# A hybrid decoder trunk: where the branch-gate projections run, beside the RWKV scan or behind it

## The chip, the cores and the metric

The kernel runs on one core of a Trainium2 chip. The metric is the device time of one execution in microseconds. Engines are named as in the profile: PE (TensorE matmul), PEld (TensorE weight load), DVE (VectorE), ACT (ScalarE), POOL (GpSimd), SP (the engine that issues the DMAs).

## The reference

Two layers on 1024 tokens of width 1024 (float32), then a final RMSNorm. In each layer one input projection feeds three causal mixers of width 512 and three branch gates of width 1024; the branches are multiplied by their gates, summed, projected and added to the residual:

```python
proj = h @ w_in
pool_u, pool_g, q, k, v, ret_g, rw, rw_g, gate_logits = jnp.split(proj, points, axis=-1)
o_pool = causal_pool_mixer(pool_u, pool_w, pool_scale) * jax.nn.silu(pool_g)
o_ret = retention(q, k, v, positions, ret_norm_g) * jax.nn.silu(ret_g)
o_rwkv = rwkv7_time_mix(rw, ...) * jax.nn.silu(rw_g)
branches = jnp.stack([o_pool, o_ret, o_rwkv], axis=2)
y = jnp.einsum('btnw,nwd->btnd', branches, w_branch)
gates = jax.nn.sigmoid(gate_logits.reshape(B, T, N_BRANCHES, D))
merged = jnp.sum(gates * y, axis=2)
return x + gate * (merged @ w_out)
```

The RWKV mixer carries a 64x64 state per head through the sequence: `S = S*w + (S a) b + v k`, read out by `r`. It has 8 heads, and is the only part that is serial over the whole sequence.

## The kernel before

Everything is kept transposed, channels on the 128 partitions and tokens along the free dimension, in two halves of 512 tokens. The dense products are computed as three float32r products each (high by high, high by low, low by high), so the input projection of one **item**, 128 output channels of all 1024 tokens, is 2 halves x 8 input tiles x 3 = 48 matmuls of 128x512, all written to the tag `acc` (three PSUM banks). Items are named `lora`, `k`/`r`/`v` (the RWKV inputs of one pair of heads; three together are `RW(i)`), `rq`/`rk`/`rv`/`rg` (retention of one head, `RT(i)`), `pu`/`pg` (one pool group, `PL(g)`), `wg` (RWKV's SiLU gate), `gate n d` (branch gate n, output tile d: 24 per layer, `GT`), `br n d` (branch product for two output tiles, 48 matmuls, `BR`) and `out`.

The RWKV mixer is done for a pair of heads at a time, four pairs a layer, in the generator `rwkv_task`: `prepare` and `scores` for each half (elementwise work on DVE and ACT, small products on PE, into `BK`, `AR`, `G`), the inversion of 32x32 triangles on DVE (`invert`, L924), small products that combine them (`m1`, `m2`, L972 to L993), and then 16 steps of 64 tokens (L1000). A step goes PE (`two<-S,AR`, L1010), DVE (`xst`, L1020), PE (`ch<-xst,G`, L1026), DVE (`Z`, L1027), PE (`ch<-Z,BKt`, L1029), DVE (`S`, L1032), and the next step needs the new `S`. `prog[(l, i)]` is unset until pair i's scores are done, then counts its steps. The pairs run one after the other.

Two orders decide what stands beside what. The **program order** is made while the kernel is traced: small tasks sit in lanes (`norm`, `post`, `rwkv`, `mix`, `ada`), each with a due time on an estimated clock; `mm1` traces the dense matmuls one by one, each advances the clock, and after each `pump` (L415) lets every lane advance whose due time has come. So a scan step's small products stand in the program between as many dense matmuls as the estimate says that its other engines need. On top of this the **framework's scheduler** orders each engine's instructions: in its own model of time it takes the earliest line of the program whose operands and buffers are ready, so that later instructions can move ahead into a hole. On the chip each engine runs its instructions in that order.

Which dense item comes next is said by the planner `plan_layer` (L471), asked one item ahead by `wprep` (L512), which also loads and splits the weights (`wr`, then `wh` on ACT and `wl` on POOL, three buffers each). In the kernel before it yields `lora` and `RW(0)`, then as soon as pair `done` has begun its steps `RW(done+1)` and `RT(done)`, pool items as `done` grows, and in between, whenever none of these may come yet, items of the list `pre`: 24 branch-gate items. Such an early gate item goes through `evac` (L1147): tanh on ACT into `gsg`, and a store to `gd` in DRAM. Gate items that were not reached come behind the scan.

Behind the scan (`merge`, L499, consumed from L1511) the list `seq` is worked off without its early items. A gate item there goes straight from PSUM into a tile `gs` (15 buffers, borrowed from the tags `ri`, `rk`, `vp`, `cs`); early gates are loaded back into such tiles by `prefetch` (L1489). A `br` item multiplies its product with the gate and adds it to `mrg`; its operand, the branch's output, is loaded and split by `load_o` (L1468, tiles `ol`, `oG`, `olo`). Then `out` follows.

Of the kernel before, what the change touches and what calls it, by code (L numbers as in the profile page):

```python
# [54 lines left out]
def RW(h):  # L55
    return [("k", h), ("r", h), ("v", h)]


def RT(h):
    return [("rq", h), ("rk", h), ("rv", h), ("rg", h)]  # L60


def PL(g):
    return [("pu", g), ("pg", g)]


def GT(n, *ds):
    return [("gate", n, d) for d in ds]


def BR(n, *ds):
    return [("br", n, d) for d in ds]
# [24 lines left out]
def trunk_kernel(ctx, tc, xT, cvec, pos, vecs, consts, w_ada, w_all, pool_w, lora_w, out):  # L97
# [15 lines left out]
    def gtile(s):  # L113
        return gp.tile([P, 32 * P + 8], F32, tag="G", name=nm(s))
# [3 lines left out]
    def nm(s):  # L118
        uid[0] += 1
        return f"{s}_{uid[0]}"  # L120
# [34 lines left out]
    def r8(s):  # L155
        return rp.tile([P, 2048], F32, tag="r8", name=nm(s))
# [153 lines left out]
    names = ("norm", "post", "rwkv", "mix", "ada")  # L310
    lanes = {k: deque() for k in names}
    due = {k: 0.0 for k in names}
    clock = [0.0]
# [55 lines left out]
    def advance(k):  # L369
        q = lanes[k]  # L370
        if not q:
            return False
        settle()
        try:
            dt = next(q[0])
        except StopIteration:
            q.popleft()
            dt = 0.0
        due[k] = max(due[k], clock[0]) + (dt or 0.0)
        return True  # L380
# [34 lines left out]
    def pump():  # L415
        for k in names:
            while lanes[k] and due[k] <= clock[0] and advance(k):
                pass
# [34 lines left out]
    prog = {}  # L453
# [5 lines left out]
    def kept(l):  # L459
        return l + 1 == L  # L460

    def out_order(l, part):
        return (2, 3, 0, 4, 5, 1, 6, 7) if kept(l) and part else range(8)
# [3 lines left out]
    def plan():  # L467
        for l in range(L):
            yield from ((l, it) for it in plan_layer(l))

    def plan_layer(l):  # L471
        yield from [("lora",)] + RW(0)
        pools = deque(PL(i) for i in range(4))
        pre = deque(GT(0, *range(8)) + GT(1, 0, 1, 4, 5, 6, 7) + GT(2, 2, 3, 4, 5, 6, 7, 0, 1) + GT(1, 2, 3))
        late = deque([("wg", 0), ("wg", 1), ("wg", 2)])
        done = 0
        while done < 4 or prog.get((l, 3), 0) < 13 or pools or halves[l] < 15:
            if done < 4 and prog.get((l, done), -1) >= 0:
                done += 1
                if done < 4:  # L480
                    yield from RW(done)
                yield from RT(done - 1)
            elif pools and 4 - len(pools) <= done and len(lanes["mix"]) < 2:
                yield from pools.popleft()
            elif pre or late:
                q = late if late and (done == 4 and prog.get((l, 3), -1) >= 0 or not pre) else pre
                it = q.popleft()
                early[l].add(it)
                yield it
            elif pools:  # L490
                yield from pools.popleft()
            elif done < 4:
                done += 1
                if done < 4:
                    yield from RW(done)
                yield from RT(done - 1)
            else:
                break
        yield ("merge",)  # L499
        seq = GT(1, 2, 3) + BR(0, 0, 2, 4, 6) + [("wg", 0), ("wg", 1)]  # L500
        seq += GT(1, 0, 1) + BR(1, 0, 2) + GT(1, 4, 5) + BR(1, 4)
        seq += [("wg", 2), ("wg", 3)] + GT(1, 6, 7) + BR(1, 6)
        seq += GT(2, 0, 1) + BR(2, 0) + GT(2, 2, 3) + BR(2, 2) + GT(2, 4, 5, 6, 7) + BR(2, 4, 6)
        yield from [it for it in seq if it not in early[l]]
        for part in range(2 + (l + 1 == L)):
            yield from [("out", d, part) for d in out_order(l, part)]
# [4 lines left out]

    def wprep(big=False):  # L512
        for l, it in planner:
            if it != ("merge",):
                break
            wready.append((it, None))
        else:
            return
        t = None
        if it[0] == "out" and it[1] >= 2 and kept(l):  # L520
            if it[2]:
                wready.append((it, keep_w[it[1]]))
                return
            if it[1] < 6:
                t = r8("wout")
            else:
                if it[1] == 6:
                    keep_w["G"] = gtile("wG")
                t = keep_w["G"][:, 2048 * (it[1] - 6) : 2048 * (it[1] - 5)]
        elif big:  # L530
            t = r8("wbig")
        parts = []
        for j in range(2):
            if t is not None:
                o = j * D
                hi, lo = t[:, o : o + HF].bitcast(F32R), t[:, o + HF : o + D].bitcast(F32R)
            else:
                hi = wp.tile([P, HF], F32R, tag="wh", name=nm("wh"), bufs=3)
                lo = wp.tile([P, HF], F32R, tag="wl", name=nm("wl"), bufs=3)
            raw = wp.tile([P, HF], F32, tag="wr", name=nm("wr"), bufs=3)  # L540
            nc.sync.dma_start(out=raw, in_=w_all[l, ITEMS.index(it[:2] if it[0] == "out" else it), j])
            split(raw, hi, lo)
            parts.append((hi, lo))
        if it[0] == "out":
            keep_w[it[1]] = parts
        wready.append((it, parts))
# [14 lines left out]
    def split(src, hi, lo, eng=nc.gpsimd):  # L561
        nc.scalar.copy(hi, src)  # L562
        eng.tensor_tensor(lo, src, hi.bitcast(F32), op=ALU.subtract)  # L563
# [723 lines left out]
    with tc.manual_schedule(engines={ET.PE, ET.DVE, ET.Activation, ET.Pool}):  # L1287
# [108 lines left out]
        both(6, V)  # L1396
        both(7, V)
        wprep(True)
        wprep()
        mms(0, 6)  # L1400
        mms(0, 7)
# [7 lines left out]
    for i in range(3):  # L1409
        evac(FIRST[i], acc6[1][i], 1)  # L1410
    wprep()
    setup_rest()
    add("mix", rope_tables())
    late_ada = [(0, g) for g in (6, 7)] + [(1, g) for g in range(8)]

    for l in range(L):
# [10 lines left out]
        def in_tile2(ws):  # L1427
            pss = [acc_ps(), acc_ps()]
            for j in range(2):
                for h in range(2):  # L1430
                    mm3(pss[h], ws[j], hs[h][4 * j : 4 * j + 4], j == 0, j == 1)
            return pss
# [9 lines left out]
                    evac(it, in_tile(ws, h), h)  # L1442
        while wready[0][0] != ("merge",):
            it, ws = wready.popleft()
            wprep()
            for h, ps in enumerate(in_tile2(ws)):
                evac(it, ps, h)
# [63 lines left out]
        while wready[0][0][0] != "out":  # L1511
            it, ws = wready.popleft()
# [49 lines left out]
        for part, (h, sl) in enumerate(parts):  # L1562
# [3 lines left out]
            for i, d in enumerate(out_order(l, part)):  # L1566
                it, ws = wready.popleft()
# [147 lines left out]
```

## Time and profile before

| | before |
|---|---|
| median of 2 runs | 2431.43 us (2431.26 to 2431.59) |
| profiled execution, span | 2431.3 us |
| PE busy | 2353.2 us (97%), 13312 matmuls |
| DVE, POOL, ACT busy | 1313.5, 820.8, 799.9 us |
| DMA | 220.51 MB, 28.5% of 16 engines |
| stores to `gd`, loads from it | 74 and 74, of 256 KB |

The profiled execution's span and its runs' times agree within 0.3 us, so spans and times can be compared directly. In the rows of the profile a line number is that of the kernel; L445 is the helper that every matmul goes through, so matmuls are told apart by the tiles they write and read, and not by line. `x` counts instructions; behind the bar stand the union of their busy time, the mean duration of one in ns, and the idle time of the engine ahead of them with what ended it. The 74 stores are 37 items of the 48 in two layers: 11 gate items came behind the scan already.

### The profile page before, as it was taken

The page shows a single profiled execution, that of the slowest core. Times are in us where ns is not written, and L with a number is a line of the kernel's source. Part 1 is how long each engine was busy: PE and PEld are TensorE (multiplying, and loading weights), DVE is VectorE, ACT ScalarE, POOL GpSimd, SP SyncE. Part 2 cuts the span into 40 slices and gives each one's busy share as a digit, 9 for nine tenths or more (in the row PEclk, how much of TensorE's full clock was granted, in tenths as well). Part 3 has the DMA queues.
Part 4 walks back from the last instruction along what each step waited for, and adds up shares of the span by engine and source line. Part 5 has one row for each costly group of instructions (what it writes and reads, how often), then busy time and mean ns, then how long its engine had stood idle before and what let it go on. Part 6 is the DMA issues. An engine that isn't in the chain of part 4 may idle for free. (4 is left out here: it accounts for less than half of the span.)

```text
span 2431.3 us, 34768 instructions
## 1 busy us (share of the span) xinstructions
PE 2353.2 (97%) x13312; PEld 1925.5 (79%) x13312; DVE 1313.5 (54%) x2564; ACT 799.9 (33%) x1481; POOL 820.8 (34%) x729
## 2 busy tenths in 40 slices
PE   5989999999999999999999999999999999999998
PEld 4768878878887888777877887888787888878888
DVE  7665477367468542457455646745644674322244
ACT  5542333333234223112453324323322323212243
POOL 4321232232232424364442222323313332455241
PEclk9999999999999999999999999999999999999999
DMA  7132112111213225666431211211211222543152
GB/s 252 49 109 70 40 40 75 53 39 53 67 52 109 75 70 173 190 202 206 153 114 44 79 40 40 83 37 44 67 58 39 67 73 71 186 130 96 52 152 79
DMA packets 122487, 220.51 MB, mean 91 GB/s; under 512 B 13904, under 2 KB 17232, under 8 KB 122320
## 3 DMA queue, kind: packets, MB, share of 16 engines
q1 hardware_dynamic: 122320, 218.29, 28.5%
q8 instruction: 104, 1.70, 0.3%
q14 instruction: 63, 0.52, 0.1%
HBM read 172.89 MB, written 45.35 MB: 90 GB/s over the span
## 5 line engine op out<-in xcount | busy, mean ns | idle before, releaser
L563 POOL TENSOR_TENSOR wl<-wr,wh 128x512 fp32r<-128x512 f32 x342 | 452.5, 1324 | 1150.8 <-ACT wh L562 1082.0
L445 PE MATMUL acc<-hhi,wh 128*128 128x512 f32 x2000 | 808.6, 404 | 9.6 <-ACT gsg L1150 8.2
L445 PE MATMUL acc<-hhi,wl 128*128 128x512 f32 x2000 | 811.4, 406 | 1.5 <-POOL r L1070 1.5
L445 PE MATMUL acc<-hlo,wh 128*128 128x512 f32 x2000 | 809.6, 405 | 0.0
L445 PEld LDWEIGHTS acc<-hhi,wh 128*128 128x128 f32 x2000 | 380.6, 190 | 78.9 <-ACT gsg L1150 9.4
L445 PEld LDWEIGHTS acc<-hhi,wl 128*128 128x128 f32 x2000 | 380.8, 190 | 70.5 <-POOL r L1070 2.0
L445 PEld LDWEIGHTS acc<-hlo,wh 128*128 128x128 f32 x2000 | 380.7, 190 | 66.1 <-issue 0.7
L562 ACT CAST wh<-wr 128x512 fp32r<-128x512 f32 x342 | 211.8, 620 | 619.2 <-PE acc L445 436.4
L445 PE MATMUL acc<-olo,wh 128*128 128x512 f32 x384 | 155.3, 405 | 5.9 <-POOL olo L563 5.9
L445 PE MATMUL acc<-oG,wh 128*128 128x512 f32 x384 | 155.0, 405 | 3.1 <-ACT oG L562 1.7
L445 PE MATMUL acc<-oG,wl 128*128 128x512 f32 x384 | 153.0, 400 | 0.0
L1032 DVE SCALAR_TENSOR_TENSOR S<-ch,pc,SP 64x64 f32<-64x64 f32 x256 | 72.5, 283 | 98.8 <-PE ch L445 96.1
L1020 DVE TENSOR_TENSOR xst<-two,MT 64x128 f32<-64x128 f32 x128 | 37.6, 293 | 157.8 <-PE two L445 143.8
L1008 ACT ACTIVATE SP<-S,pc 128x128 f32<-128x128 f32 x128 | 51.5, 402 | 208.1 <-DVE S L1032 198.0
L445 PEld LDWEIGHTS acc<-olo,wh 128*128 128x128 f32 x384 | 73.9, 192 | 25.3 <-POOL olo L563 8.9
L445 PEld LDWEIGHTS acc<-oG,wh 128*128 128x128 f32 x384 | 73.4, 191 | 22.8 <-ACT oG L562 2.9
L445 PEld LDWEIGHTS acc<-oG,wl 128*128 128x128 f32 x384 | 73.8, 192 | 17.8
L1539 DVE SCALAR_TENSOR_TENSOR gs<-gs,acc 128x512 f32<-128x512 f32 x64 | 43.5, 683 | 78.5 <-PE acc L445 78.5
L939 DVE TENSOR_TENSOR tm<-MT,two 64x30 f32<-64x30 f32 (+14 forms) x240 | 76.5, 319 | 12.9 <-ACT two L932 5.6
L945 DVE TENSOR_TENSOR two<-two,tm 64x30 f32<-64x30 f32 (+14 forms) x240 | 78.9, 329 | 7.3
L1027 DVE COPY Z<-ch 64x128 f32<-64x128 f32 x128 | 36.0, 282 | 82.1 <-PE ch L445 81.6
L1537 DVE SCALAR_TENSOR_TENSOR mrg<-gs,acc 128x512 f32<-128x512 f32 x32 | 22.0, 687 | 107.6 <-PE acc L445 105.4
(287 smaller groups left out, 3690.7 us busy)
## 6 DMA issues: line engine op xcount, KB each, us to landing
wr<-in_w_all SPq DMA_DIRECT2D x364, 256.0 KB, 2.7
gd<-gsg SPq DMA_DIRECT2D x74, 256.0 KB, 2.0
gs<-gd SPq DMA_DIRECT2D x74, 256.0 KB, 2.9
wada<-in_w_ada SPq DMA_DIRECT2D x70, 256.0 KB, 3.2
ol<-od SPq DMA_DIRECT2D x64, 256.0 KB, 3.0
ringG<-in_w_ada SPq DMA_DIRECT2D x26, 256.0 KB, 4.9
x<-in_xT SPq DMA_DIRECT2D x16, 256.0 KB, 4.8
od<-po SPq DMA_DIRECT2D x16, 256.0 KB, 2.0
```

The costliest lines, as they stand in the source:

```text
L445: return nc.tensor.matmul(out, lhsT=lhsT, rhs=rhs, start=start, stop=stop, **kw)
L562: nc.scalar.copy(hi, src)
L563: eng.tensor_tensor(lo, src, hi.bitcast(F32), op=ALU.subtract)
L939: nc.vector.tensor_tensor(pr, L3[:, i + 1 :, i : i + 1].to_broadcast([64, n, i]), M3[:, i : i + 1, 0:i].to_broadcast([64, n, i]), op=ALU.mult,
L945: nc.vector.tensor_tensor(M3[:, i + 1 :, 0:i], M3[:, i + 1 :, 0:i], pr, op=ALU.add)
L1008: nc.scalar.activation(SP, S, AF.Copy, scale=pcc)
L1020: nc.vector.tensor_tensor(xst[0:64, :], cy[64:128, 0:P], AV[:, c * P : (c + 1) * P], op=ALU.add)
L1027: nc.vector.tensor_copy(Z[0:64, c, :], ch[0:64, 0:P])
L1032: nc.vector.scalar_tensor_tensor(Sn[rw, rw], ch[rw, P + 64 * hd : P + 64 * hd + 64], pc[rw, c : c + 1], SP[rw, rw], op0=ALU.mult, op1=ALU.add,
L1537: nc.vector.scalar_tensor_tensor(m, s, 1.0, ps, op0=ALU.add, op1=ALU.mult)
L1539: nc.vector.scalar_tensor_tensor(s, s, 1.0, ps, op0=ALU.add, op1=ALU.mult)
```

## The change

The list `pre` is empty. Where nothing else may come, the planner now yields `idle`, for which no dense item is traced: the estimated clock jumps to the next due time of a lane, the lanes advance, and the planner is asked again. `wg` i may come as soon as pair i+1 has begun its steps. The 24 gate items of a layer stand in `seq`, each ahead of the branch products that use it, so that none is stored to `gd` or loaded from it.

```diff
-        pre = deque(GT(0, *range(8)) + GT(1, 0, 1, 4, 5, 6, 7) + GT(2, 2, 3, 4, 5, 6, 7, 0, 1) + GT(1, 2, 3))
+        pre = deque()
...
-            elif pre or late:
-                q = late if late and (done == 4 and prog.get((l, 3), -1) >= 0 or not pre) else pre
-                it = q.popleft()
+            elif late and prog.get((l, late[0][1] + 1), -1) >= 0:
+                it = late.popleft()
                 early[l].add(it)
                 yield it
-            elif pools:
+            elif pools and 4 - len(pools) <= done:
                 yield from pools.popleft()
-            elif done < 4:
-                done += 1
-                if done < 4:
-                    yield from RW(done)
-                yield from RT(done - 1)
+            elif any(lanes[k] for k in ("rwkv", "mix")):
+                yield ("idle",)
             else:
                 break
         yield ("merge",)
-        seq = GT(1, 2, 3) + BR(0, 0, 2, 4, 6) + [("wg", 0), ("wg", 1)]
-        seq += GT(1, 0, 1) + BR(1, 0, 2) + GT(1, 4, 5) + BR(1, 4)
+        seq = GT(0, 0, 1, 2, 3) + BR(0, 0, 2) + GT(0, 4, 5, 6, 7) + BR(0, 4, 6)
+        seq += [("wg", 0), ("wg", 1)] + GT(1, 0, 1, 2, 3) + BR(1, 0, 2) + GT(1, 4, 5) + BR(1, 4)
         seq += [("wg", 2), ("wg", 3)] + GT(1, 6, 7) + BR(1, 6)
...
-            if it != ("merge",):
+            if it not in (("merge",), ("idle",)):
                 break
             wready.append((it, None))
+            if it == ("idle",):
+                return
...
             it, ws = wready.popleft()
+            if ws is None:
+                clock[0] = max(clock[0], min(due[k] for k in names if lanes[k]))
+                pump()
+                wprep()
+                continue
             wprep()
```

## The prediction

> **What bounds the kernel now.** I read the page first (who is busy), then the busy time by stretches of one head pair, then single instructions of one scan step.
>
> ```profile
> span 2431.3 us, 34768 instructions
> PE 2353.2 (97%) x13312; PEld 1925.5 (79%) x13312; DVE 1313.5 (54%) x2564; ACT 799.9 (33%) x1481; POOL 820.8 (34%) x729
> PE   5989999999999999999999999999999999999998
> L445 PE MATMUL acc<-hhi,wh 128*128 128x512 f32 x2000 | 808.6, 404 | 9.6 <-ACT gsg L1150 8.2
> L445 PE MATMUL acc<-olo,wh 128*128 128x512 f32 x384 | 155.3, 405 | 5.9 <-POOL olo L563 5.9
> gd<-gsg SPq DMA_DIRECT2D x74, 256.0 KB, 2.0
> gs<-gd SPq DMA_DIRECT2D x74, 256.0 KB, 2.9
> ```
>
> TensorE is busy in every slice behind the start, and has 78 us of idle in all. The span is the time: the two runs took 2431.26 and 2431.59 us, so the sum below starts from 2431.3 with nothing around it. Busy is not bound by itself, since durations of pipelined matmuls overlap. What a dense matmul (128x512) costs is read where there is nothing else:
>
> ```profile
> 2200.00:2250.00 50.00, 50.00 (x219) 40.91 (x218) 10.61 (x14) 13.13 (x23) 26.68 (x21) 1.00 0.34 106
> ```
>
> 50.0/219 is 0.228 us; I use 0.227 us (the next 50 us hold 221). One projection item is 2 halves of 24 matmuls, 10.9 us.
>
> The RWKV scan is a serial chain beside this. One head pair of layer 1, in four stretches: its preparation and scores (A), the inversion, the rest until the first scan step, and the 16 steps. First all work, then only the matmuls into `acc` (the dense ones):
>
> ```profile
> 1477.70:1548.60 70.90, 68.99 (x403) 56.34 (x403) 48.80 (x90) 28.94 (x52) 22.17 (x22) 1.00 0.17 54
> 1548.60:1579.40 30.80, 30.23 (x175) 24.31 (x175) 25.87 (x67) 10.75 (x17) 8.03 (x7) 1.00 0.26 86
> 1579.40:1603.40 24.00, 24.00 (x209) 19.89 (x208) 7.62 (x5) 5.59 (x10) 4.60 (x6) 0.93 0.19 55
> 1603.40:1676.20 72.80, 72.69 (x436) 59.48 (x434) 32.91 (x87) 20.03 (x50) 22.45 (x22) 1.00 0.13 41
> ...
> 1477.70:1548.60 70.90, 52.68 (x205) 36.90 (x205) 2.71 (x4) 5.31 (x9) 1.00 0.17 54
> 1548.60:1579.40 30.80, 25.08 (x105) 19.17 (x105) 0.00 (x0) 2.97 (x5) 1.00 0.26 86
> 1579.40:1603.40 24.00, 19.87 (x79) 15.40 (x78) 1.50 (x2) 1.52 (x3) 0.93 0.19 55
> 1603.40:1676.20 72.80, 70.37 (x240) 41.09 (x239) 11.28 (x16) 4.21 (x8) 1.00 0.13 41
> ```
>
> The columns are length, then busy time and count of PE, PEld, DVE, ACT, POOL. A pair takes 198.5 us, with 629 dense matmuls: 46.5 us of them in A and 96 us behind it (424 x 0.227), 142.8 us together. TensorE's other work of the pair is 198.5 - 142.8 = 55.7 us, 24 us of it in A. So TensorE is full, and the question is whether the chain could go faster with less beside it.
>
> **The chain without filler.** One scan step, TensorE's small matmuls and then VectorE's part:
>
> ```profile
> 648.89 0.38 PE L445 MATMUL two<-S,AR 128*128 128x128 f32 x2
> 650.03 0.40 PE L445 MATMUL ch<-xst,G 128*65 128x64 f32 x4
> 651.25 0.38 PE L445 MATMUL ch<-Z,BKt 128*128 128x128 f32 x2
> 652.17 0.40 PE L445 MATMUL two<-Z,G 128*65 128x64 f32 x4
> 652.70 0.38 PE L445 MATMUL two<-S,AR 128*128 128x128 f32 x2
> ...
> 649.38 0.29 DVE L1020 TENSOR_TENSOR xst<-two,MT 64x128 f32<-64x128 f32 x1 [0.92 <-PE two L445]
> 650.46 0.28 DVE L1027 COPY Z<-ch 64x128 f32<-64x128 f32 x1 [0.79 <-PE ch L445]
> 651.67 0.58 DVE L1032 SCALAR_TENSOR_TENSOR S<-ch,pc,SP 64x64 f32<-64x64 f32 x2 [0.92 <-PE ch L445]
> ```
>
> The step takes 3.81 us. VectorE answers TensorE 0.11, 0.03 and 0.04 us after it ends. TensorE answers VectorE after 0.36 (649.67 to 650.03), 0.51 and 0.45 us, since dense matmuls that stand ahead in its order are run first. With answers of some 0.06 us both ways the step is 2.7 us, 16 of them 43 us, with the ends of the stretch 46 instead of 72.8. Between inversion and scan:
>
> ```profile
> 1579.41 2.08 DVE L948 STREAM_TRANSPOSE MT<-two 32x1024 f32<-32x1024 f32 x1
> 1581.50 4.05 DVE L920 STREAM_TRANSPOSE G<-two 32x1024 f32<-32x1024 f32 x2
> ...
> 1603.44 0.29 DVE L1020 TENSOR_TENSOR xst<-two,MT 64x128 f32<-64x128 f32 x1 [12.56 <-PE two L445]
> ```
>
> VectorE is done at 1585.6, the scan begins at 1603.4: of these 24 us some 9 to 10 are needed. The inversion is VectorE's own (25.9 of 30.8 us busy): 27 us. A has 48.8 us of VectorE work in 70.9 us: I take 50, between 46 and 70.9. The pair needs about 50 + 27 + 9 + 46 = 132 us by its chain.
>
> **The change part by part.**
>
> 1. *Moved.* 74 stored halves are 37 items, 74 x 24 x 0.227 = 403 us of TensorE work, 34 us of a middle pair (629 matmuls become 480: RW 3 items, RT 4, pool 2, one `wg`). Behind the scan they come back at the same price: +403 behind, and up to -403 in the scan. Their weight loads and splits move along; one item needs two casts on ScalarE and two subtractions on GpSimd in 10.9 us, which is hidden there as it was.
>
> 2. *Removed.* The 74 stores and 74 loads, and the waits that come with them. TensorE waited 8.2 us for `gsg`, whose buffers are held by stores, and 5.9 us for `olo`, where a branch product followed the last one directly; gates now stand between. Between 0 and -17; I take -13. The transfers themselves hid behind TensorE.
>
> 3. *New idle in a middle pair.* Work is 109 (480 x 0.227) + 55.7 = 165 us, the chain alone 132, so with perfect placement TensorE would still be full. But the dense items of a pair are released when its scores are done, and are dealt out between the chain's steps at the old rate: 96 us of them last until the scan's end. A then has only what is left. Dense matmuls can be moved ahead of their place in program order when TensorE has a hole, since the framework's scheduler orders each engine's instructions by readiness; what bounds that is the three `acc` banks, 3 x 24 x 0.227 = 16.3 us. So A lasts 50 us, 24 its own, 16 pulled ahead, 10 idle; behind it 93 us of dense work are left, at the old rate 125 us. The pair takes 175 instead of 198.5, so of the 34 us removed 24 are got back and 10 are new idle. Bounds: 3 us where evacuated banks serve again within A; without any pulling ahead 13 us overflow from 96 to 109, A is 20 us at the old pace and 36 without filler, the pair is 184 and 19 us are idle. Six such pairs: 60, between 18 and 114.
>
> 4. *The ends of each scan.* The first pair's A has the pool item (21.8 us) and what is pulled ahead, and no mixer tasks: 0 to 15 us idle. The last pair has only `RT(3)` and `wg` 2, 240 matmuls, where it had
>
> ```profile
> 1945.70:2085.00 139.30, 118.00 (x429) 78.16 (x428) 12.36 (x18) 7.72 (x13) 0.98 0.24 74
> ```
>
> 429, or 97 us. 54 us are 56% of them; the other 44% of the stretch (61 us) run at the chain's rate, some 40 us, 18 of which are TensorE's own; the first gates can be pulled into the other 22, as far as `acc` and the gate tiles' buffers reach. 0 to 20 us idle. I take 6 each, 4 x 6 = 24; between 0 and 70.
>
> 5. *The clock.* Where TensorE does little, its granted clock falls; in the kernel before it does so in the small products ahead of the scan:
>
> ```profile
> 622.90:629.70 6.80, 6.80 (x94) 5.25 (x93) 0.69 (x1) 2.40 (x4) 1.27 (x1) 1.00 0.26 80
> 629.70:636.50 6.80, 6.80 (x65) 5.92 (x63) 0.00 (x0) 1.15 (x2) 0.00 (x0) 0.50 0.00 0
> 636.50:643.30 6.80, 6.80 (x43) 5.64 (x42) 2.47 (x7) 2.17 (x5) 1.29 (x1) 1.00 0.21 77
> ```
>
> One such stretch more in each of eight pairs costs 3.4 us (half of 6.8) where dense work lies in it, and nothing where TensorE is idle anyway: 0 to 27 for one stretch, 54 for two. I take 14.
>
> Sum: 2431.3 - 13 + 60 + 24 + 14 = 2516 us. Low ends: 2431.3 - 17 + 18 = 2432. High ends: 2431.3 + 114 + 70 + 54 = 2669.
>
> The Trainium skill, "TensorE: Matmul & The Clock Gate" (HAM oscillation), says that idle gaps of more than about 3.4 us put the array back to half clock, after which the next matmuls start cold. The trace agrees in kind (0.50 for 6.8 us), and by that rule A would be cold in most of its length; that is rival 2.
>
> **Rivals.**
>
> 1. *The scan is filled all the same* (not slower): matmuls pulled ahead cover A, banks are reused as soon as the next pair's `k` tiles may be written, and the chain's 132 us stay below 165 us of work. For it: the 33 us between 132 and 165. Against it: nothing dense is released in A, and TensorE runs in order, so a small matmul placed too early holds up the dense ones behind it. Time: 2431.3 - 17 + 6 x 3 + 4 x 2 + 8 = 2448; it decides where A's idle and cold time stay under about 6 us a pair, since 2% is 48.6 us for eight.
>
> 2. *Cold A* (slower by more): with gaps in A the clock is at 0.5 for most of it, so that 24 + 16 us of TensorE work there take up to 80 instead of 40 and A is 70 again. Per pair 20 us more, 160 for eight: 2516 - 14 + 160 = 2662. Against it: A holds small matmuls throughout, and its 403 matmuls leave few gaps of several us.
>
> 3. *The chain keeps its pace*: if VectorE's and ScalarE's own order, not TensorE's queue, set 3.81 us a step and 198.5 us a pair, all that is moved is added: 2431.3 - 13 + 403 = 2821. Against it: the three answers of 0.36 to 0.51 us in the step, and 12.56 us in which VectorE waited ahead of the scan.
>
> That the change doesn't do what it says could show in the last pair alone, where gates are pulled back into the scan; it is counted in part 4.
>
> **How the numbers follow.** The forecast has 0.58, rival 1 0.26, rival 2 0.10, rival 3 0.06. The predicted time is the forecast's, 2516 us. The range reaches from rival 1's time, less 8 us, to rival 2's: 2440 to 2660; it leaves out rival 3 and the outer parts of the others, under 2 in 10. 2% is 48.6 us, about what a measurement of this kernel can tell from no change: 2383 to 2480. Faster than 2383 would need 48 of TensorE's 78 idle us to go: 0.02. Within: rival 1 for the most part, 0.23. Slower: 0.75.
>
> **What would show it.** Right: no `gd` transfers; scans whose middle pairs follow each other in some 175 us; a step under 3 us where no dense matmul is left beside it; TensorE's busy share lower in the slices of A only, and the stretch behind each scan longer by about 200 us. Wrong: pairs still 198 us apart (rival 3), pairs of 165 us (rival 1), a clock of 0.5 through A (rival 2); or TensorE idle behind the scan, where I put none.

## The result, and the profile after

The changed kernel takes 2595.99 us (2595.44 to 2596.53) against 2431.43: 1.0676 times before (1.0658 to 1.0693), 164.6 us slower. The forecast was 2516 us, with a range of 2440 to 2660. The page after, its head and the rows that answer to those shown of before:

```profile
span 2594.7 us, 34583 instructions
PE 2456.7 (95%) x13312; PEld 2012.5 (78%) x13312; DVE 1304.6 (50%) x2564; ACT 804.9 (31%) x1481; POOL 817.8 (32%) x729
PE   5999999999896999999999999999999979999998
PEclk9999999999797999999999999998987989999999
L445 PE MATMUL acc<-hhi,wh 128*128 128x512 f32 x2000 | 808.7, 404 | 0.1
L445 PE MATMUL acc<-olo,wh 128*128 128x512 f32 x384 | 151.7, 395 | 0.0
```

TensorE runs the same 13312 matmuls. Its idle time rose from 78 to 138 us (2594.7 - 2456.7), by 60; its busy time rose by 103.5 us, from 2353.2 to 2456.7. Together that is the whole difference of the spans, 163.4 us. The clock row (PEclk, the share of TensorE's full clock that was granted, in tenths) has 7s and 8s where before had only 9s, late in each layer's scan. The waits for `gsg` and `olo` are gone, and no `gd` row is left among the DMA issues.

The two answers on the granted clock, of after and of the kernel before, give the clock's part:

```profile
die 0 (median of its cores): 2594.7 us, clock 0.949
...
die 0 (median of its cores): 2431.3 us, clock 0.985
```

In both traces the recorded clock is either 1.0 or 0.5, so a mean of 0.949 is some 265 us at half clock; before it was some 75. Summed over the trace, TensorE was busy in 216.5 us of these stretches, before in 62.9. Half of the difference, 77 us, is what the clock took if every matmul takes twice as long at half clock; small products take 1.6 times as long (rows below), and with that for all it would be 58. So 58 to 77 us is an estimate. That leaves 27 to 46 us of the rise in busy time. They fit small products that stand alone, whose time no longer overlaps that of dense ones: TensorE was busy with no matmul into `acc` for 268.7 us before (2353.2 - 2084.5) and for 421.5 us after (2456.7 - 2035.2), and of the rise of 153 us, 122 lie at half clock and 31 at full clock. So the loss is 60 us idle, some 58 to 77 us clock, and the rest lost overlap. This is bookkeeping of one trace: at full clock some of the busy time would have become idle time.

By place, in windows of layer 1: the four stretches of the first middle pair (preparation and scores A, inversion, up to the first step, steps), the second middle pair whole, the last pair whole; first all work, then dense matmuls alone:

```profile
1551.00:1610.40 59.40, 53.74 (x281) 41.23 (x281) 48.79 (x82) 24.24 (x44) 19.98 (x21) 0.97 0.13 42
1610.40:1647.00 36.60, 36.60 (x202) 30.78 (x201) 32.33 (x77) 9.36 (x15) 12.71 (x11) 1.00 0.13 38
1647.00:1656.40 9.40, 8.83 (x141) 7.77 (x140) 5.90 (x5) 2.92 (x5) 1.56 (x2) 0.77 0.21 53
1656.40:1720.90 64.50, 62.22 (x408) 51.63 (x407) 28.31 (x86) 20.46 (x49) 13.17 (x15) 0.95 0.12 34
1720.90:1900.20 179.30, 173.69 (x1073) 141.74 (x1072) 115.98 (x252) 58.96 (x117) 53.29 (x52) 0.94 0.15 45
1900.20:2089.20 189.00, 168.66 (x992) 135.97 (x991) 123.77 (x261) 54.17 (x107) 49.84 (x40) 0.85 0.15 48
...
1551.00:1610.40 59.40, 31.73 (x122) 23.14 (x121) 4.33 (x6) 3.88 (x8) 0.97 0.13 42
1656.40:1720.90 64.50, 49.45 (x155) 26.36 (x154) 1.38 (x2) 3.94 (x7) 0.95 0.12 34
1720.90:1900.20 179.30, 131.77 (x481) 87.57 (x480) 16.84 (x24) 10.37 (x20) 0.94 0.15 45
1900.20:2089.20 189.00, 101.62 (x372) 71.02 (x371) 13.70 (x20) 5.54 (x10) 0.85 0.15 48
```

The middle pairs take 169.9 and 179.3 us where they took 198.5, with 5.7 us idle in the first one's A (59.4 - 53.7). The stretch ahead of the steps fell from 24 to 9.4 us. The last pair is the bad one: 372 dense matmuls, a clock of 0.85, 20 us idle.

What small products cost by themselves is seen at its end, where no dense work is left (TensorE in order of time, columns start and length, in brackets the idle time ahead):

```profile
2074.06 0.41 PE L445 MATMUL two<-S,AR 128*128 128x128 f32 x2
2074.93 0.45 PE L445 MATMUL ch<-xst,G 128*65 128x64 f32 x4 [0.46 <-DVE xst L1018]
2075.75 0.49 PE L445 MATMUL ch<-Z,BKt 128*128 128x128 f32 x2 [0.38 <-DVE Z L1025]
2076.98 0.49 PE L445 MATMUL two<-S,AR 128*128 128x128 f32 x2 [0.51 <-DVE S L1030]
...
2080.30 0.80 PE L445 MATMUL two<-S,AR 128*128 128x128 f32 x2 [0.31 <-DVE S L1030]
2081.55 0.70 PE L445 MATMUL ch<-xst,G 128*65 128x64 f32 x4 [0.46 <-DVE xst L1018]
2082.62 0.80 PE L445 MATMUL ch<-Z,BKt 128*128 128x128 f32 x2 [0.38 <-DVE Z L1025]
2084.26 0.79 PE L445 MATMUL two<-S,AR 128*128 128x128 f32 x2 [0.41 <-DVE S L1030]
...
2097.67 1.11 PE L451 MATMUL yt<-cst,yc 128*128 128x128 f32 x4 [9.86 <-POOL yc L707]
2098.43 0.78 PE L445 MATMUL acc<-hhi,wh 128*128 128x512 f32 x1
```

A bare step is 2.92 us (2074.06 to 2076.98). A few us later the clock is halved, the small products take 1.6 times as long (0.80 for 0.49, 0.70 for 0.45), and the step 3.96 us (2080.30 to 2084.26): the bare chain at half clock is slower than the 3.81 us that it took amid dense matmuls. The last row but one is a stall of 9.86 us (9.88 in layer 0): TensorE's next instruction waits for the last head's norm on GpSimd, and the first gate matmul, the last row, runs behind it.

### The profile page after: what moved, and what is told of

It is laid out like the page before. It is cut to its first block, busy times and chain, and to the rows that moved or that the text cites. A ratio compares the mean times of both kernels' runs of the same rounds, so it can differ in the third digit from the quotient of the medians.

```text
span 2594.7 us, 34583 instructions
## 1 busy us (share of the span) xinstructions
PE 2456.7 (95%) x13312; PEld 2012.5 (78%) x13312; DVE 1304.6 (50%) x2564; ACT 804.9 (31%) x1481; POOL 817.8 (32%) x729
## 5 line engine op out<-in xcount | busy, mean ns | idle before, releaser
L1525 ACT ACTIVATE gs<-acc 128x512 f32<-128x512 f32 x96 | 56.8, 594 | 91.3 <-PE acc L445 91.3
```

What stands on the lines that cost most here:

```text
L1525: nc.scalar.activation(gate_tile((n, d, h)), ps, AF.Tanh, scale=0.5)
```

## The experiments

Theory 1: beside each pair stands less dense work than its chain needs as cover, most of all beside the last one; there TensorE is partly idle and partly at half clock, since small products alone don't keep the clock up. Rivals: the chain's own engines hold it; the order behind the scan or the early `wg` items cost the time; idle time alone, without the clock, explains it.

**Spreading the same dense work.**

```diff
+            clock[0] += slow[0]
             pump()
...
+        slow[0] = 68.0
         while wready[0][0] != ("merge",):
...
+        slow[0] = 0.0
         drain("rwkv", "mix")
```

> The changed kernel, with one number added to the estimated clock: each dense matmul traced in the scan stage advances it by 68 ns more (30%), so that the chain is given more progress per dense matmul and the same dense items reach further, into the next pair's preparation (A). Theory 1 (the dense items of a pair run out behind its scan, A is left with idle time and with a low clock): middle pairs of 170 to 179 us come near TensorE's own 165, the time at half clock falls from 266 us to under 150, and the time from 2596 to 2490 to 2550 us. Rival (the chain without filler is held by its own engines and by small products that stand too early in TensorE's order): no gain, 2580 to 2640 us.

2517.53 us, 78 less than the change, 1.0352 of before (1.0337 to 1.0367). The page and the clock:

```profile
PE 2405.8 (96%) x13312; PEld 1953.6 (78%) x13312; DVE 1291.8 (51%) x2564; ACT 804.1 (32%) x1481; POOL 815.5 (32%) x729
...
die 0 (median of its cores): 2513.0 us, clock 0.978
...
1819.90:2005.90 186.00, 131.85 (x473) 85.33 (x473) 15.06 (x22) 8.27 (x14) 0.97 0.18 56
```

As theory 1 said: 51 us less busy time for the same matmuls, 31 us less idle (107 left), the half-clock time down to some 113 us, and the middle pairs of layer 1 at 162 and 169 us. The third row, the dense matmuls in the last pair of layer 1, shows how: 473 stand beside it instead of 372, since the others' dense work was put off into it.

**More room for gates that are pulled ahead.**

```diff
-        gs_free = [t_ri] * 7 + [t_rk] * 4 + [t_vp] * 2 + [t_cs] * 2
+        gs_free = [t_rk] * 4 + [t_vp] * 2 + [t_ri] * 7 + [t_cs] * 2
```

> The changed kernel, with the gate tiles borrowed first from the tags rk and vp, which are free when the last pair scans, and from ri after them. Theory: the two stalls of 9.9 us at the end of the scans come from gate items that were pulled ahead and hold all three acc banks, since their ri tiles are still the scan's; with free tiles more gates are pulled ahead, the stalls go, and the time falls by 10 to 30 us, to 2566 to 2586. Rival (the stall is TensorE's order alone, the transposes of yc standing ahead of the first gate): within 3 us of 2596.

2562.41 us, 34 less, a little more than expected. The dense matmuls in the last pair's steps, of after and of this run:

```profile
2022.10:2089.20 67.10, 32.16 (x99) 17.70 (x99) 1.36 (x2) 1.19 (x2) 0.90 0.19 60
...
2001.00:2067.00 66.00, 44.63 (x142) 24.85 (x143) 1.37 (x2) 3.56 (x6) 0.97 0.22 69
```

43 more dense matmuls, of gates, were pulled into the scan, and the clock of this stretch rose from 0.90 to 0.97. So the gate tiles did hold them back; that gates without a tile kept the three `acc` banks meanwhile fits, but no row shows it. The stall ahead of `yt` did not go, as the theory said it would: it fell from 9.88 and 9.86 us to 5.58 and 5.95. The rest of it fits the rival, TensorE's order.

**Less beside the scan.** The `late` list of the planner is emptied, so that all `wg` items follow the scan.

> The changed kernel, with no wg item beside the scan either: all four come behind it (6 items, 65 us of TensorE work, leave the two scans). Theory 1 (what leaves the scan is given back only in part): 2615 to 2640 us. Rival (the scan is bound by TensorE's work, so that it shortens by what leaves): 2590 to 2600 us.

2625.2 us, 29 more. 65 us of work left the scans and 36 of them were got back, as theory 1 says; a scan bound by TensorE would have got back all.

**All gates back, the rest as changed.**

```diff
-        pre = deque()
+        pre = deque(GT(0, *range(8)) + GT(1, 0, 1, 4, 5, 6, 7) + GT(2, 2, 3, 4, 5, 6, 7, 0, 1) + GT(1, 2, 3))
...
+            elif pre:
+                it = pre.popleft()
+                early[l].add(it)
+                yield it
             elif any(lanes[k] for k in ("rwkv", "mix")):
                 yield ("idle",)
```

> The changed kernel, with the gate list of before in place of the idle step: where nothing else may come, an early gate item does, stored to DRAM and loaded back, and idle only when the list is empty. The three wg items and the order behind the scan stay as changed. Theory 1 (the whole loss is TensorE work missing beside the chain): 2420 to 2445 us, as before, and the time at half clock near before's 77 us. Rival (the early wg items or the new order behind the scan cost part of it): 2460 us or more.

2450.4 us, 146 of the 164.6 us recovered; the clock is 0.983. The run lies between the two expectations, nearer the first: 18 us more than before (1.0070, 1.0055 to 1.0085). Candidates are the `wg` items ahead of the gates and the order behind the scan, but neither is shown. By place the whole loss lies in layer 0: its scan ends 9 us later than before, the first scan step of layer 1 comes 20 us later, and behind that nothing is lost, though layer 1 has the same edits. Its cause stays open.

**Spread and room together.**

> The two edits together: 68 ns more clock per dense matmul beside the scan, and gate tiles from rk and vp first. Theory 1 (the gate tiles mattered because the last pair had no dense work left at its end; with the work spread it has some, and the stall is gone already): within 8 us of 2517.5. Rival (two separate losses): 2517.5 less the 34 us that the gate tiles gave alone, 2475 to 2495 us.

2519.79 us: no further gain, as theory 1 says. The room mattered because the last pair lacked dense work, and spread work had filled that end already. The stall itself was not gone with the spread alone, though: it is 6.34 and 6.29 us there.

**More spread.**

> The same with 100 ns instead of 68. Theory 1 (a pair has 165 us of TensorE work and the old rate deals out dense work for 198: the right stretch is about a third, beyond it nothing more is gained): within 15 us of the run with 68 ns, half clock within 30 us of its. Rival (the less dense work stands beside the chain, the faster the chain): another 20 us or more off.

2547.31 us, 27 slower than with 68 ns, so neither: too thin a spread leaves work over that comes back behind the scan. Against the run before it, the time at half clock rose by some 13 us. Up to layer 0's last step, and from layer 1's first step to its last, 23 us were won; the rest of the kernel has 145 dense matmuls more and grew by 50 us.

**Matmuls of no use as cover.** Two 128x512 products into an unread `acc` bank at each idle step of over 0.3 us.

> The changed kernel with two dense matmuls of no use (128x512, from tiles that are there, into an acc bank that nobody reads) at each idle step of more than 0.3 us: some 690 of them, 156 us of TensorE work at full clock. Theory 1 (about 100 of the 164 us lost are matmuls at half clock, which falls where small products stand alone): time at half clock falls from 266 us to under 150, and the time stays within 25 us of 2596 although 156 us of work are added. Rival (the loss is idle time and the clock hardly matters): half clock stays above 200 us and the time rises by 60 us or more.

2639.88 us, 44 more than the change. Page and clock:

```profile
PE 2552.7 (97%) x13938; PEld 2085.1 (79%) x13938; DVE 1294.6 (49%) x2564; ACT 803.6 (30%) x1481; POOL 815.4 (31%) x729
...
die 0 (median of its cores): 2642.3 us, clock 0.976
```

626 matmuls were added, 142 us at 0.227. The half-clock time fell to some 130 us, as theory 1 said, but the time rose by more than it said and by less than its rival. By the spans (2642.3 and 2594.7), 94 of the 142 us cost nothing: 48 went into idle time (138 to 90), and 46 were won as busy time (2456.7 to 2552.7 - 142 = 2411). So the clock is a true part of the loss, and "about 100" was too much for it. TensorE's busy time at half clock fell by 101 us, from 216.5 to 115.4, for 46 us won; at that rate the 154 us of it that the change had added cost some 70, within the 58 to 77 estimated above.

**Gates beside the last pair alone.** As the run with all gates back, with `elif pre and done >= 3`.

> The changed kernel with early gates (stored and loaded as before) in place of the idle step only from the third pair's scan on, so beside the last pair's preparation, inversion and steps. Theory 1 (half of the loss lies with the last pair of each layer, which has 240 dense matmuls where it had 429, stays at half clock and ends with a stall): 2490 to 2530 us. Rival (the loss is spread evenly over the pairs): 2550 us or more.

2501.81 us, 94 of the 164.6 us recovered with 19 of 48 gate items beside the scan.

```profile
gd<-gsg SPq DMA_DIRECT2D x38, 256.0 KB, 2.1
...
1847.50:2058.40 210.90, 173.67 (x657) 119.58 (x657) 13.73 (x20) 13.87 (x24) 0.99 0.25 80
```

The second row is the last pair of layer 1. It lasts 210.9 us instead of 189.0, but with 657 dense matmuls instead of 372: 65 us of work in 22 us. Its clock is 0.99 instead of 0.85. More than half of the loss is got back here.

**Both, with the spread ended when gates begin.** `slow[0] = 0.0` from the third pair's steps on, then gates as in the run before.

> The changed kernel, spread by 68 ns per dense matmul until the third pair of a layer begins its steps, then at the old rate with early gates (stored and loaded) in place of the idle step. Theory 1 (the two losses are separate by place: the first three pairs' dense work ran out too soon, the last pair had too little; the spread alone shortened the first three pairs by 28 and 42 us, the gates beside the last one gave 94): 2425 to 2445 us, no slower than 2% against before with half the gates stored. Rival (the gain of the spread lay at the last pair too, or the spread costs the gates their place): 2470 us or more.

2509.17 us: the rival was right, the two gains don't add up. I read the spread's gain and that of the gates as one and the same, dense work for the last pair; that fits, since the gates kept their place (36 stores instead of 38), but the run doesn't separate this from a cost of the spread itself.

**The same, the switch one pair later.**

> The same with the switch one pair later: spread until the last pair begins its steps, early gates beside its inversion and steps alone. Theory 1 (with the spread the last pair's preparation is covered by its own dense items, as the run with the spread showed, so gates are needed behind it alone): within 15 us of the run before it, with some 20 stores less. Rival (the last pair's preparation needs gates too): 20 us or more slower.

2509.88 us with 20 stores (10 items) instead of 36: as expected, with the spread 10 items are enough for the same time.

**A smaller spread.**

> As the first of the two, with 45 ns in place of 68. Theory 1 (68 ns is about the ratio 198 to 165 plus what is pulled ahead, and less lets the dense work run out again): within 10 us of the first, on the slower side if at all. Rival (the spread puts small products too early, so that less of it is better): 10 us or more faster, and below 2431 us.

2497.55 us (1.0269, 1.0249 to 1.0290), 12 faster than with 68 ns, but still slower than before: the rival's half. With 38 stores it is level with the gates beside the last pair alone (2501.81 us, also 38): their runs overlap. No version with so few early gates did better.

**More filler in the kernel before.** There 15 ns are taken off per dense matmul.

> The kernel before, with each dense matmul beside the scan counted 15 ns shorter on the estimated clock, so that some 7% more dense matmuls stand between the chain's steps and more gate items fit beside the scan. Theory 1 (what idle time before has beside the scan, some 30 us, are small products that stand too early; more filler covers part of them, and where TensorE is full a longer scan costs nothing): 2412 to 2429 us. Rival (the chain already has what it needs, and a longer scan only moves gate items): within 4 us of 2432 or slower.

2439.93 us, 1.0031 of before (1.0020 to 1.0042), with 86 stores instead of 74: its rival was right. I found no version faster than before.

Taken together: that the chain's own engines hold the time falls with the spread, which takes 78 us off with the same work. The early `wg` items and the order behind the scan can account for 18 us at most, the distance left with all gates back. And idle time alone does not explain the loss, since useless dense matmuls won back 46 us of busy time beside the idle time that they filled.

## Why the prediction was right, and where it was off

The direction and the main mechanism held: TensorE's order, not the chain's engines, set the old pace; the chain got faster, and less was got back than was moved. The sum was 80 us short: the clock was mis-sized, and one term, the overlap that small products lose when they stand alone (27 to 46 us), was not in it at all.

*Part 1, moved.* 37 gate items left the scans, but three `wg` items a layer come beside the scan in their place. I counted these in the pairs and not in the 403 us. The net work moved was 31 items (1488 dense matmuls, 338 us), and the stretches behind the scans grew by 175 us (layer 0) and 163 us (layer 1), not by some 200. The scans shortened by 177 together.

*Part 2, removed waits.* Right: 8.2 and 5.9 us became 0.1 and 0.0. But I did not see the new wait ahead of `yt`, 9.9 us a layer, which takes it all back (19.7 us for both layers).

*Part 3, middle pairs.* 175 us forecast, 169.9 and 179.3 measured. The chain's pieces were near: a bare step 2.92 us against 2.7; 9.4 us ahead of the steps against 9. A was 59.4 us and not 50, with 122 dense matmuls (27.7 us) instead of 16 us pulled ahead, and 5.7 us idle instead of 10. What follows A took 110.5 us and not 125, so that the sum came out near 175 is in part luck: the two errors cancel.

*Part 4, the ends.* I gave the last pair 6 us idle; it had 20 and the stall behind it. Half of the 20 lay in its steps: there the gates could not be pulled ahead far enough, for lack of gate tiles, as the run with other tiles showed (8.6 us idle in the last steps of layer 1 became 3.8). The other half lay in its A, which that run left as it was.

*Part 5, the clock.* This is the term that was mis-sized: 14 us, with 54 as its far bound; the trace gives 58 to 77. I counted one more cold stretch a pair, of the length seen before (6.8 us). But cold stretches grew with the length without dense work: there are 25 of up to 34.1 us where there were 14 of up to 6.9, and of the 190 us more at half clock, some 106 lie with the last pair of each layer. Idle time, which I took for the greater term (84, less part 2), rose by 60.

The rivals: the scan was not filled all the same (1). The chain did not keep its pace (3). Rival 2, a cold A, was half right: its time, 2662, was too long, for A was at half clock in 28 and 30 of its 75 us with the last pairs, and in less with the others.

On the page of the Trainium skill that I cited, "TensorE: Matmul & The Clock Gate" (HAM oscillation): it explains the half clock by idle gaps of more than about 3.4 us. The trace bears that out in part. Of the last pairs' stretches at half clock four began while TensorE waited 4.11 to 5.49 us for VectorE or GpSimd, and these four hold 78 of their 120 us. One of the two longest of the four, in layer 0, with the wait (the row in brackets), all work behind the wait, and the whole stretch as all work and as dense alone:

```profile
689.55 2.07 PE L445 MATMUL two<-AR,BK 64*128 64x128 f32 x8 [5.49 <-DVE BK L856]
...
689.55:713.30 23.75, 23.75 (x118) 19.95 (x119) 18.69 (x25) 6.71 (x10) 5.11 (x4) 0.50 0.11 34
...
686.00:713.30 27.30, 23.75 (x118) 19.95 (x119) 22.24 (x31) 6.91 (x11) 5.58 (x5) 0.50 0.10 29
...
686.00:713.30 27.30, 3.90 (x9) 3.13 (x10) 6.16 (x9) 0.00 (x0) 0.50 0.10 29
```

What the gap does not explain is the length. Behind it TensorE was busy for 23.75 us without a break, with 118 matmuls, 9 of them dense, and the clock stayed at 0.50; it came back 3.9 us after the dense ones set in (709.40 to 713.30). Nor does every fall need such a gap. At the end of the last pair (rows of 2074 to 2084 above) the clock fell with no gap of over 0.51 us in those rows. And the row of 629.7 to 636.5, which the prediction took as agreeing with the page, has no idle time at all: 56 of its 65 matmuls are products of 32x32.

## What to carry to other kernels

Work that "only fills" an engine beside a serial chain may be what keeps that engine fast: when it is moved, count the idle time and the clock of what stays behind. Look for the place with the least filler left, here the last of four pairs: 19 of 37 early items put there gave back more than half of the loss. And before a busy engine is called full, subtract what its own work needs; here the same 13312 matmuls were 103.5 us more "busy" at no more work.

## What the runs showed of the hardware that was not expected

That the clock can fall and stay low while small products keep TensorE busy (6.8 us at 0.50 with no idle time before the change; 23.75 us at 0.50 with no idle time after it, behind a wait of 5.49 us), so that a serial chain of them can be faster amid dense matmuls (3.81 us a step) than alone at half clock (3.96 us), though slower than alone at full clock (2.92 us).
